# The opening of a diffusion trunk: the first norm's modulation maps computed in two halves of their outputs

## Chip, cores and metric

The kernel runs on one core of a Trainium2 chip. The metric is the device time of one execution in microseconds; lower is better. Where a profile is quoted, it is that of one execution, and its times count from the start of that execution's span.

## What is computed

Two layers of a transformer trunk over 1024 latent tokens and 256 context tokens, with 1024 channels. Layer 0 mixes tokens by neighbourhood attention, layer 1 by sliding-window attention; each layer ends with a gated ConvFFN. The part that matters here is the very first: the modulated norm ahead of layer 0's attention, and the projection to q, k and v behind it.

```python
silu_c, silu_cc = jax.nn.silu(c), jax.nn.silu(c_ctx)
for i in range(DEPTH):
    mod = silu_c @ w_mod[i] + b_mod[i]          # (6*D): shift, scale, gate, twice
    mod_c = silu_cc @ w_mod[i] + b_mod[i]       # the same map for context tokens
    sh1, sc1, gt1, sh2, sc2, gt2 = jnp.split(mod[:, None, :], 6, axis=-1)
    ...
    h = modulate(rmsnorm(x, g_attn[i]), sh1, sc1)        # y * (1 + scale) + shift
    hc = modulate(rmsnorm(ctx, g_attn[i]), sh1c, sc1c)
    ...
    q, k, v = attn_inputs(h, w_in, gq, gk, n_kv)         # h @ w_qkv, head norms
```

So before the first projection the kernel needs two maps of w_mod for layer 0, shift and scale: 1024 inputs by 2048 outputs, 8.4 MB of float32.

## The kernel before

**Layout.** Activations lie with channels on the 128 partitions: 8 channel blocks (`KT`), block k holding channels 128k to 128k + 127, tokens along the free dimension. Tokens come in three chunks (`CH`, line 419): chunk 0 and 1 are 512 latent tokens each, chunk 2 the 256 context tokens. The input is `xs[c]`, the modulated norm `h[c]`. Every operand of a big matmul is split in two float32r parts, hi (a rounded copy, made by ACT or DVE) and lo (the rest, a subtraction on DVE or GpSimd), and each product is three matmuls: hi by hi, lo by hi, hi by lo. In the trace chunk 2's parts are `h0chi` and `h0clo`, chunk 0's `h0hi` and `h0lo`; chunk 1's are made later, by `plan_norm`, from the tile that the trace calls `x` too and with sums named `sums`.

**Weights of the projection** come as slabs (class `Slabs`, lines 509 to 545): slab i of a head pair holds channel blocks 2i and 2i + 1, 384 KB, rows of 3 KB. `load` fetches it into a ring of three buffers (`rpool`, tag `raw`), `hi` makes `whi` on ACT, `lo` makes `wlo` on DVE or GpSimd. The first head pair needs slabs 0 to 3; slab 3 takes the buffer of slab 0, and so its load waits for slab 0's lo part. The rings of `whi` and `wlo` have four places each; the input of chunk 2 lies in two places of `wlo` (line 906: blocks 0 to 3 in one, 4 to 7 in the other), so two of the four slabs' lo parts wait until chunk 2's blocks are done with them.

**The opening** (lines 903 to 975) is ordinary program text under Tile's scheduler. That scheduler lays down one queue per engine at build time: by program order among what it takes to be ready. From the first planner's run on (`sc.run()`, line 1264) the order is fixed by hand instead: `Sched` computes an order of all operations from costs and keys, and `InOrder` (line 67) ties each engine's instructions to it. All instructions that go through `InOrder` carry its line, L79, in the trace, so they are told apart by tile names.

The opening's program order before:

1. Loads on SyncE's queue (SP): chunk 2's input in two transfers, biases and gains, chunk 0's input in four, then `wm` for kt = 0 to 7: each 128 rows of both maps, 1 MB, each row 8 KB in one piece.
2. `stats(2)`, then `stats(0)`: squares on ACT, their sum on DVE (`nsum`), the mean by TensorE (`nps<-invd,nsum`), the inverse root by GpSimd and three small DVE operations, its broadcast over partitions by TensorE (`nps<-dg,ones`), and the multiplication of the input by it, block by block (`x<-x,nps`).
3. The maps: for each kt and each of the two maps `mod_mm` (line 316), four matmuls of 256 outputs into four strips of an accumulator, `mod`; 64 matmuls, which the trace counts as 128 instructions. ACT copies each accumulator (`modsb`), TensorE transposes it (`modt`), DVE adds the bias and folds the gain into the scale (`modc`): `mod_finish`, line 299.
4. Loads: slabs 0 to 2, chunk 1's input in four transfers (x1), `c_row`, `cv`.
5. `apply(2)`: per block x * scale + shift (on ACT for even blocks, on DVE for odd ones), the hi copy (on the other of the two), and the lo part on DVE, or on GpSimd for blocks 3 and 7. Then `slabs.ahead(4)`: load where not done, hi and lo of the four slabs, lo of 0 and 2 on DVE, of 1 and 3 on GpSimd. Then `apply(0)`.

**What comes behind.** `plan_na_qkv` (line 1019) projects token tiles of 128 in the order 8, 9 (context), 0, 1, and so on (`ORDER`, line 423); each is 24 matmuls of 384 outputs, `mm`, in the order of the channel blocks. The first tile thus needs slab 0 for blocks 0 and 1, slab 1 for 2 and 3, and so on. Chunk 1's statistics (`sums`, then `pt<-invd,sums` on TensorE) stand in the same hand-made order, behind the first latent tiles. None of that part's text or costs is touched by the change.

Of the kernel before, what the change touches and what calls it, by code (L numbers as in the profile page):

```python
# [34 lines left out]


WBUFS = 4

class Weave:

    def __init__(self):
        self.jobs = []

    def add(self, gen, rank=0):

        self.jobs.append((rank, gen))
        self.jobs.sort(key=lambda j: j[0])

    def tick(self, n=1):
        for _ in range(n):
            left = []
            for j in self.jobs:
                try:
                    next(j[1])
                    left.append(j)
                except StopIteration:
                    pass
            self.jobs = left  # L60

    def drain(self):
        while self.jobs:
            self.tick()


class InOrder:

# [20 lines left out]
class Sched:  # L89
# [6 lines left out]
                                       pool=(0.15, 0.08, 0.06, 0.1), dma=(0.0, 0.0, 0.0, 0.0)).items()  # L96
# [145 lines left out]
def trunk_kernel(ctx, tc, xperm, xseq, cc, crow, wmod, wmodt, bmod, gnorm, na_wqkv, na_gqk, na_bias, na_wo,  # L242
# [3 lines left out]
    act, dve, pool, pe, dma = [InOrder(tc, e) for e in (nc.scalar, nc.vector, nc.gpsimd, nc.tensor, nc.sync)]  # L246
# [45 lines left out]
    W = Weave()  # L292

    def split(dst_hi, dst_lo, src):
        act.activation(dst_hi, src, AF.Copy)
# [213 lines left out]
    class Slabs:  # L509
# [17 lines left out]

        def get(self, i):
            return [a.rearrange("p (k c) -> p k c", k=2) for a in self.w[i]]

        def ahead(self, n):

            self.n_ahead = n
            for i in range(n):
                if i not in self.raw:
                    self.load(i)
                self.hi(i)
                self.lo(i, "pool" if i % 2 else "dve")
# [362 lines left out]
    with tc.tile_pool(name="x0", bufs=1, reuse_waits="tile") as xp, \  # L901
# [16 lines left out]
        x_load(2, 2)  # L918
        dma.dma_start(bmod_t, bmod)
        dma.dma_start(gn, gnorm)  # L920
        accs = [ps.tile([P, 512], F32, tag="mod", name=f"mod{v}", bufs=2) for v in range(2)]
        raws = []
# [6 lines left out]
        def stats(c):  # L929

            n = CH[c][1]
            nm = Norm(xs[c], n, lw, lambda: ps.tile([P, 512], F32, tag="n", name="nps", bufs=2), dve)
            for k in range(KT + 1):
                nm.square(k)
                yield
            yield from nm.rstd()
            for k in range(KT):
                dve.tensor_tensor(out=xs[c][:, k, :], in0=xs[c][:, k, :], in1=nm.bc[:, :n], op=ALU.mult)
                yield

        def apply(c):
            r = int(c == 2)
            for k in range(KT):
# [8 lines left out]
                yield  # L952
# [24 lines left out]
    fin = ph.enter_context(tc.tile_pool(name="fin0", bufs=1, reuse_waits="tile"))  # L977
    wk = ph.enter_context(tc.tile_pool(name="wk0", bufs=2, reuse_waits="tile"))
# [1526 lines left out]
```

## Time and profile before

| | |
|---|---|
| median of 3 runs | 2797.7 us (2796.82 to 2798.07) |
| the profiled execution | 2796.63 us, of which the span is 2794.9 us |
| mean granted TensorE clock | 0.99 |
| busy: TensorE matmul, VectorE (DVE), ScalarE (ACT), GpSimd (POOL) | 97%, 82%, 61%, 14% of the span |
| DMA | 385.30 MB, mean 138 GB/s |

The busy shares are means over stages with different limits. The page also has the span in 40 slices of 70 us, with a digit for tenths busy; the timeline lists an engine's instructions as start, duration, engine, line, operation, `out<-in`, shapes and count, and in brackets the idle time before it with what ended it. An entry with a count is several instructions in a row. SPq rows are DMA issues: their start is when SyncE got to issue the transfer.

### The profile page before, as it was taken

The page shows a single profiled execution, that of the slowest core. Times are in us where ns is not written, and L with a number is a line of the kernel's source. Part 1 is how long each engine was busy: PE and PEld are TensorE (multiplying, and loading weights), DVE is VectorE, ACT ScalarE, POOL GpSimd, SP SyncE. Part 2 cuts the span into 40 slices and gives each one's busy share as a digit, 9 for nine tenths or more (in the row PEclk, how much of TensorE's full clock was granted, in tenths as well). Part 3 has the DMA queues.
Part 4 walks back from the last instruction along what each step waited for, and adds up shares of the span by engine and source line. Part 5 has one row for each costly group of instructions (what it writes and reads, how often), then busy time and mean ns, then how long its engine had stood idle before and what let it go on. Part 6 is the DMA issues. An engine that isn't in the chain of part 4 may idle for free.

```text
span 2794.9 us, 43305 instructions
## 1 busy us (share of the span) xinstructions
PE 2713.8 (97%) x15496; PEld 2336.0 (84%) x15496; DVE 2290.5 (82%) x5034; ACT 1704.0 (61%) x3111; POOL 385.1 (14%) x550
## 2 busy tenths in 40 slices
PE   5999999998999999999999999999999999999999
PEld 4899999987799988888888888888877788888887
DVE  6888888887778688777886889989978988888767
ACT  4777777776456555556564557677754666566433
POOL 2111111112000000000010035656620000000000
PEclk9999999999999999999999999999999999999999
DMA  6233343335555543333475641233243223324655
GB/s 259 75 121 122 122 127 105 114 114 164 213 168 186 182 140 108 130 121 129 139 253 169 200 142 57 72 96 105 84 155 106 80 98 113 106 88 160 232 173 188
DMA packets 145264, 385.30 MB, mean 138 GB/s; under 512 B 21269, under 2 KB 34069, under 8 KB 143641
## 3 DMA queue, kind: packets, MB, share of 16 engines
q1 hardware_dynamic: 145048, 382.55, 42.0%
q8 instruction: 121, 1.98, 0.3%
q14 instruction: 95, 0.77, 0.1%
HBM read 315.50 MB, written 66.99 MB: 137 GB/s over the span
## 4 chain that ended last, share of the span: by engine, by line
PE 65%; DVE 5%; issue 2%; POOL 1%; DMA 1%; ACT 1%; POOLq 0%; DVEq 0%; SPq 0%; ACTq 0%
PE ua L79 17%; PE dn L79 15%; PE uc L79 13%; PE mm L79 5%; PE ud L79 4%; PE oacc L79 3%; PE pt L79 2%; PE dnc L79 2%; PE pv L79 2%; PE s L79 2%; DVE S L79 1%; DVE x L79 1%; POOL qa L79 0%; DVE wlo L79 0%; DMA c_dram<-cx 0%
## 5 line engine op out<-in xcount | busy, mean ns | idle before, releaser
L79 ACT ACTIVATE whi<-wraw 128x512 fp32r<-128x512 f32 (+1 forms) x264 | 211.9, 803 | 153.6 <-PE uc L79 57.7
L79 DVE TENSOR_TENSOR wlo<-wraw,whi 128x512 fp32r<-128x512 f32 (+1 forms) x264 | 239.9, 909 | 48.5 <-ACT whi L79 48.1
L79 ACT ACTIVATE S<-S,m 128x640 f32<-128x640 f32 (+3 forms) x288 | 221.0, 768 | 59.6 <-DVE m L79 40.1
L79 PE MATMUL dn<-ghi,whi 128*128 128x512 f32 x616 | 239.9, 390 | 0.0
L79 PE MATMUL dn<-ghi,wlo 128*128 128x512 f32 x616 | 239.7, 389 | 0.0
L79 PE MATMUL dn<-glo,whi 128*128 128x512 f32 x616 | 239.6, 389 | 0.0
L79 ACT ACTIVATE whi<-s 128x1024 fp32r<-128x1024 f32 (+1 forms) x120 | 113.2, 943 | 192.8 <-PE uc L79 128.7
L79 POOL TENSOR_TENSOR qy<-qv,mhalf 128x4 f32<-128x4 f32 (+2 forms) x120 | 137.9, 1150 | 545.7 <-DVE qv L79 512.0
L79 PE MATMUL pt<-idr,S 128*128 128x128 f32 x1280 | 189.7, 276 | 7.8 <-DVE S L79 2.9
L79 ACT ACTIVATE ghi<-graw 128x512 fp32r<-128x512 f32 x154 | 96.0, 629 | 151.7 <-PE dn L79 94.9
L79 PE MATMUL mm<-whi,h0hi 128*128 128x384 f32 x512 | 180.5, 353 | 1.6 <-ACT qraw L79 1.6
L79 PEld LDWEIGHTS pt<-idr,S 128*128 128x128 f32 x1280 | 151.5, 142 | 27.4 <-issue 9.8
L79 PE MATMUL mm<-wlo,h0hi 128*128 128x384 f32 x512 | 172.7, 337 | 0.0
L79 DVE TENSOR_TENSOR glo<-graw,ghi 128x512 fp32r<-128x512 f32 x154 | 105.6, 694 | 80.1 <-ACT ghi L79 47.3
L79 ACT ACTIVATE pt<-pt 128x512 f32<-128x512 f32 (+2 forms) x241 | 124.5, 536 | 55.5 <-PE pt L79 53.9
L79 PE MATMUL pv<-pt,v 128*64 128x256 f32 (+1 forms) x1376 | 154.3, 370 | 0.0
L79 DVE TENSOR_TENSOR wlo<-s,whi 128x1024 fp32r<-128x1024 f32 (+1 forms) x120 | 129.6, 1080 | 23.4 <-ACT whi L79 23.1
L79 PE MATMUL ua<-t12hi,whi 128*128 128x512 f32 x352 | 139.0, 395 | 4.9 <-ACT t12hi L79 4.7
L79 PE MATMUL uc<-t34h,whi 128*128 128x512 f32 x352 | 139.6, 397 | 0.5 <-ACT t34h L79 0.5
L79 PE MATMUL ua<-t12lo,whi 128*128 128x512 f32 x352 | 138.4, 393 | 1.4 <-DVE t12lo L79 1.4
L79 PE MATMUL uc<-t34l,whi 128*128 128x512 f32 x352 | 137.7, 391 | 0.9 <-DVE t34l L79 0.9
L79 PE MATMUL ua<-t12hi,wlo 128*128 128x512 f32 x352 | 137.9, 392 | 0.0
(325 smaller groups left out, 8530.6 us busy)
## 6 DMA issues: line engine op xcount, KB each, us to landing
wraw<-in_w_up_dram SPq DMA_DIRECT2D x132, 512.0 KB, 3.8
wmt<-in_wmodt_dram SPq DMA_DIRECT2D x96, 512.0 KB, 4.2
wraw<-in_w_down_dram SPq DMA_DIRECT2D x44, 512.0 KB, 4.0
graw<-g_dram SPq DMA_DIRECT2D x44, 512.0 KB, 4.8
wraw<-in_w_down_dram SPq DMA_DIRECT2D x88, 256.0 KB, 3.1
graw<-g_dram SPq DMA_DIRECT2D x66, 256.0 KB, 2.8
slab<-in_na_wqkv_dram SPq DMA_DIRECT2D x32, 384.0 KB, 3.2
woraw<-in_na_wo_dram SPq DMA_DIRECT2D x24, 512.0 KB, 5.0
```

What stands on the lines that cost most here:

```text
L79: r = f(*a, **k)
```

## The change

The two maps are computed in two halves of their outputs instead of all at once. Half 0 is outputs 0 to 511 of shift and of scale, which are the constants of channel blocks 0 to 3; half 1 the rest. The loads come half by half: for each half 8 tiles of 512 KB, each row of which is two pieces of 2 KB. Slabs 0 and 1 are loaded between the halves, slab 2 behind the second, slab 3 ahead of x1. An accumulator holds one half of both maps, and `mod_half` makes the constants of four blocks from it. `apply` takes a half: four blocks, with the lo parts after each pair. In the program's order half 0's constants, the splits of slabs 0 and 1 and blocks 0 to 3 of chunks 2 and 0 now stand ahead of the maps' second half; behind it stand blocks 4 to 7 of chunk 2, the splits of slabs 2 and 3, the x1 loads, and blocks 4 to 7 of chunk 0. The helper class `Weave` and `Slabs.ahead` go; the statistics are the same `Norm` calls, written out in line.

```diff
-        for kt in range(KT):
-            raw = xp.tile([P, 2, 1024], F32, tag="wm", name=f"wm{kt}", bufs=KT)
-            dma.dma_start(raw.rearrange("p v c -> p (v c)"), wmod[0, kt * P:(kt + 1) * P, 0:2 * D])
-            raws.append(raw)
+        def wm_load(half):
+            for kt in range(KT):
+                raws[half, kt] = xp.tile([P, 2, 512], F32, tag="wm", name=f"wm{half}{kt}", bufs=2 * KT)
+                dma.dma_start(raws[half, kt], wmod[0, kt * P:(kt + 1) * P, 0:2 * D].rearrange(
+                    "p (v c) -> p v c", v=2)[:, :, half * 512:half * 512 + 512])
+
+        wm_load(0)
+        slabs.load(0)
+        slabs.load(1)
+        wm_load(1)
+        slabs.load(2)
+        dma.dma_start(c_row, cr)
...
-        def apply(c):
+        def apply(c, half):
             r = int(c == 2)
-            for k in range(KT):
+            pend = []
+            for k in range(4 * half, 4 * half + 4):
...
-                yield
-                (pool if k % 4 == 3 else dve).tensor_tensor(out=lo, in0=x, in1=hi.bitcast(F32), op=ALU.subtract)
+                pend.append((k, x, hi, lo))
+                if k % 2:
+                    for k_, x, hi, lo in pend:
+                        (pool if k_ % 4 == 3 else dve).tensor_tensor(out=lo, in0=x, in1=hi.bitcast(F32), op=ALU.subtract)
+                    pend = []
...
-        for c in (2, 0):
-            W.add(stats(c))
-            W.drain()
-        for kt in range(KT):
-            for v in range(2):
-                mod_mm(accs[v], kt, raws[kt][:, v, :], kt == 0, kt == KT - 1)
-        for v in range(2):
-            sb = xp.tile([P, 256], F32, tag="modsb", name="modsb0", bufs=2)
-            act.activation(sb, accs[v][:, :256], AF.Copy)
-            W.add(mod_finish(0, v, sb, lambda: ps.tile([P, 512], F32, tag="modt", name="modt", bufs=2)))
-        W.drain()
-        for j in range(3):
-            slabs.load(j)
-        x_load(1, 4)
-        dma.dma_start(c_row, cr)
-        dma.dma_start(cv, conv)
-        W.add(apply(2))
-        W.drain()
-        slabs.ahead(4)
-        W.add(apply(0))
-        W.drain()
+        def mods(half, a, b):
+            for kt in range(a, b):
+                mod_mm(accs[half], kt, raws[half, kt].rearrange("p v c -> p (v c)"), kt == 0, kt == KT - 1)
+
+        def mod_half(half):
+
+            sb = xp.tile([P, 256], F32, tag="modsb", name="modsb0", bufs=2)
+            act.activation(sb, accs[half][:, :256], AF.Copy)
+            tp = ps.tile([P, 512], F32, tag="modt", name="modt", bufs=2)
+            for s in range(2):
+                pe.transpose(tp[:, s * P:(s + 1) * P], sb[:, s * P:(s + 1) * P], idf)
+            yield
+            js = slice(4 * half, 4 * half + 4)
+            for v in range(2):
+                for r in range(2):
+                    src = tp[:, :256].rearrange("p (s g q) -> p g s q", s=2, g=4)[:, 2 * v:2 * v + 2, :, r]
+                    dst = modc[:, 0, r, v, js].rearrange("p (g s) -> p g s", s=2)
+                    dve.tensor_tensor(out=dst, in0=src, in1=bmod_t[:, 0, v, js].rearrange("p (g s) -> p g s", s=2), op=ALU.add)
+            for r in range(2):
+                dve.scalar_tensor_tensor(out=modc[:, 0, r, 1, js], in0=modc[:, 0, r, 1, js], scalar=1.0,
+                                         in1=gn[:, 0, 0, js], op0=ALU.add, op1=ALU.mult)
+
...
+        mods(0, 0, 6)
+        g = nm[0].rstd()
+        next(g)
+        next(g)
+        mods(0, 6, KT)
+        m = mod_half(0)
...
+        split_slab(0, "dve")
+        split_slab(1, "pool")
+        apply(2, 0)
+        times_bc(0, nm[0], 0, 4)
+        apply(0, 0)
+        times_bc(0, nm[0], 4, KT)
+        mods(1, 0, KT)
+        for _ in mod_half(1):
+            pass
+        apply(2, 1)
+        split_slab(2, "dve")
+        split_slab(3, "pool")
         x_load(1, 4)
-        dma.dma_start(c_row, cr)
         dma.dma_start(cv, conv)
-        W.add(apply(2))
-        W.drain()
-        slabs.ahead(4)
-        W.add(apply(0))
-        W.drain()
+        apply(0, 1)
+        slabs.n_ahead = 4
```

`split_slab(i, e)` loads slab i where that isn't done, and makes its hi on ACT and its lo on engine e. `times_bc(c, nm, k0, k1)` multiplies blocks k0 to k1 - 1 of chunk c by the norm's broadcast.

More of the change, by code (lines that the diff above doesn't have):

```diff
@@ L37 @@
 WBUFS = 4
[L39 to L64, printed above, removed]
 class InOrder:
@@ L290, in trunk_kernel @@
     c_row = dpool.tile([2, D], F32, name="c_row")
-    W = Weave()
     def split(dst_hi, dst_lo, src):
@@ L529, in get @@
             return [a.rearrange("p (k c) -> p k c", k=2) for a in self.w[i]]
[L531 to L538, printed above, removed]
         def plan(self, sc, i, key, uses):
@@ L920, in trunk_kernel, with psn, times_bc, split_slab @@
         dma.dma_start(gn, gnorm)
[L921 to L941 removed]
+        raws = {}
+        def wm_load(half):
[3 more added lines that the diff above has]
+                    "p (v c) -> p v c", v=2)[:, :, half * 512:half * 512 + 512])
+        x_load(0, 4)
+        wm_load(0)
[4 more added lines that the diff above has]
+        dma.dma_start(c_row, cr)
+        def psn():
+            return ps.tile([P, 512], F32, tag="n", name="nps", bufs=2)
+        def times_bc(c, nm, k0, k1):
+            for k in range(k0, k1):
+                dve.tensor_tensor(out=xs[c][:, k, :], in0=xs[c][:, k, :], in1=nm.bc[:, :CH[c][1]], op=ALU.mult)
+        def split_slab(i, e):
+            if i not in slabs.raw:
+                slabs.load(i)
+            slabs.hi(i)
+            slabs.lo(i, e)
+        def apply(c, half):
             r = int(c == 2)
[L943 removed]
+            pend = []
+            for k in range(4 * half, 4 * half + 4):
                 x, hi, lo = xs[c][:, k, :], h[c][0][:, k, :], h[c][1][:, k, :]
@@ L965, in trunk_kernel @@
-        W.drain()
-        for j in range(3):
-            slabs.load(j)
+                pend.append((k, x, hi, lo))
[3 more added lines that the diff above has]
+                    pend = []
+        accs = [ps.tile([P, 512], F32, tag="mod", name=f"mod{half}", bufs=2) for half in range(2)]
+        def mods(half, a, b):
+            for kt in range(a, b):
+                mod_mm(accs[half], kt, raws[half, kt].rearrange("p v c -> p (v c)"), kt == 0, kt == KT - 1)
@@ new lines, in trunk_kernel @@
+        nm = {c: Norm(xs[c], CH[c][1], lw, psn, dve) for c in (2, 0)}
+        for k in range(KT + 1):
+            nm[2].square(k)
+        for _ in nm[2].rstd():
+            pass
+        times_bc(2, nm[2], 0, KT)
+        for k in range(KT + 1):
+            nm[0].square(k)
+        mods(0, 0, 6)
[4 more added lines that the diff above has]
+        m = mod_half(0)
+        next(m)
+        for _ in range(3):
+            next(g)
+        for _ in m:
+            pass
```

4 lines of the change are left out of this document (3 added, 1 removed).

## The prediction

> **What bounds the kernel now.** The page first: is TensorE the bound, and where not?
>
> ```profile
> span 2794.9 us, 43305 instructions
> PE   5999999998999999999999999999999999999999
> ```
>
> PE is full in all slices but the first (70 us), where the change lies. Windows of the trace then give the edge of that stage (columns: window, its length, busy us of PE, PEld, DVE, ACT, POOL with counts, granted clock, DMA share, GB/s):
>
> ```profile
> 0.00:60.00 60.00, 29.92 (x198) 20.72 (x199) 39.45 (x91) 27.23 (x50) 11.85 (x14) 0.89 0.77 295
> 100.00:150.00 50.00, 49.32 (x334) 46.06 (x333) 46.46 (x157) 35.74 (x83) 7.58 (x6) 1.00 0.40 127
> ```
>
> From 100 us on PE has 99%, in an order that is written out and stays. So the question is only how many us earlier PE enters its unbroken run; all behind it moves with that. The timeline of PE (start, duration, instruction, idle before and who ended it) shows the entry:
>
> ```profile
> 38.99 0.41 PE L79 MATMUL mm<-whi,h0chi 128*128 128x384 f32 x1 [2.35 <-DVE h0chi L79]
> 52.14 0.69 PE L79 MATMUL mm<-whi,h0chi 128*128 128x384 f32 x1 [4.12 <-ACT whi L79]
> 54.54 0.69 PE L79 MATMUL mm<-wlo,h0chi 128*128 128x384 f32 x1 [1.40 <-POOL wlo L79]
> 64.69 0.95 PE L79 MATMUL pt<-invd,sums 128*128 128x1 f32 x8
> ```
>
> The first matmul of the projection comes at 38.99, but the stream stops for slab 3, whose wlo GpSimd delivers at 54.49; from 54.54 PE runs on. So the entry is **the end of slab 3's split**. Why is that late? DVE, GpSimd and ACT:
>
> ```profile
> 28.49 4.87 DVE L79 TENSOR_TENSOR x<-x,nps 128x512 f32<-128x512 f32 x8 [1.65 <-PE nps L79]
> 36.25 0.24 DVE L79 TENSOR_TENSOR modc<-modt,bmod_t 128x8 f32<-128x8 f32 x2 [2.89 <-PE modt L79]
> 36.88 0.24 DVE L79 SCALAR_TENSOR_TENSOR modc<-modc,gn 128x8 f32<-128x8 f32 x2
> 37.04 0.95 DVE L79 TENSOR_TENSOR wlo<-slab,whi 128x768 fp32r<-128x768 f32 x1
> 41.04 0.28 DVE L79 CAST h0chi<-x 128x256 fp32r<-128x256 f32 x1
> 42.45 1.91 DVE L79 CAST h0chi<-x 128x256 fp32r<-128x256 f32 x1
> 52.75 2.02 DVE L79 TENSOR_SCALAR x<-x,modc 128x512 f32<-128x512 f32 x1
> ...
> 39.57 1.06 POOL L79 TENSOR_TENSOR h0clo<-x,h0chi 128x256 fp32r<-128x256 f32 x1 [14.22 <-ACT h0chi L79]
> 42.20 2.00 POOL L79 TENSOR_TENSOR wlo<-slab,whi 128x768 fp32r<-128x768 f32 x1
> 52.22 2.27 POOL L79 TENSOR_TENSOR wlo<-slab,whi 128x768 fp32r<-128x768 f32 x1 [1.81 <-issue]
> ...
> 51.26 0.83 ACT L79 ACTIVATE whi<-slab 128x768 fp32r<-128x768 f32 x1
> ```
>
> The maps are ready at 37.12 (36.88 + 0.24), and DVE is then busy without a gap to 54.77. A cast that takes 0.28 alone took 1.91 while GpSimd split a slab (42.20 to 44.20), a tensor_scalar 2.02 in the same way: DVE stalls while GpSimd runs. Slab 3's whi stood in ACT's queue behind blocks of the latent chunk. And what set 37.12? SyncE's queue:
>
> ```profile
> SPq L79 <- DMA wm<-in_wmod_dram: 18.2, 8, 3.2
> ...
> 12.98 0.33 SPq L79 DMA_DIRECT2D wm<-in_wmod_dram  x1
> 15.53 0.33 SPq L79 DMA_DIRECT2D slab<-in_na_wqkv_dram  x1
> 25.47 0.33 SPq L79 DMA_DIRECT2D x<-in_xperm_dram  x1
> 27.96 0.33 SPq L79 DMA_DIRECT2D x<-in_xperm_dram  x1
> 31.46 0.33 SPq L79 DMA_DIRECT2D x<-in_xperm_dram  x1
> 34.00 0.26 SPq L79 DMA_DIRECT2D c_row<-cr  x1
> 34.90 0.35 SPq L79 DMA_DIRECT2D cv<-in_conv_dram  x1
> 38.02 0.33 SPq L79 DMA_DIRECT2D slab<-in_na_wqkv_dram  x1
> ```
>
> SP waited eight times for a wm: each issue waits for the landing of the transfer eight places ahead. So the issues date landings: the last x0 at 12.98, the first wm at 15.53, the last at 34.00, slab 0 at 34.90; 2.49 us per 1 MB tile (25.47 to 27.96), once 3.50. Slab 3's own load (38.02) waits for slab 0's split, since it takes its buffer.
>
> **The change part by part.** *Loads.* The same 8.4 MB of wm now come as 16 tiles of 512 KB, whose rows are runs of 2 KB instead of 8. What a run's length costs, from two windows of 10 us (20 to 30, wm; 2730 to 2740, tiles of 256 KB, 2 KB per row):
>
> ```profile
> DMA packets 582, 4.24 MB, mean 424 GB/s; under 512 B 64, under 2 KB 64, under 8 KB 64
> q1 hardware_dynamic: 581, 4.24, 101.5%
> ...
> DMA packets 1588, 2.90 MB, mean 290 GB/s; under 512 B 174, under 2 KB 174, under 8 KB 1587
> q1 hardware_dynamic: 1587, 2.89, 87.9%
> ```
>
> At full share that is 424 / 1.015 = 418 GB/s against 290 / 0.879 = 330: 1.27 times the time per byte. So a 512 KB tile takes 2.49 / 2 x 1.27 = 1.58 us and a half 12.6. The window at 2730 also has stores, so the bounds are 1.24 (no price) and 1.58; I take 1.58, since nothing else in the trace moves 2 KB runs near saturation. Half 0 lands at 13.0 + 12.6 = 25.6; slabs 0 and 1, now ahead of half 1, cost 0.9 each (34.00 to 34.90): 27.4; half 1 at 40.0, or 41.0 with the one slow step (3.50 for 2.49) that the run before shows too. I take 41.0: **seven us later than the last wm now**.
>
> The Trainium skill, "DMA: Bandwidth & Descriptors", Specifications, states line rate from 512 B per transfer on; its section on small descriptors gives about 3 cycles of overhead per packet. By it 2 KB runs would cost some 3.5% more than 8 KB (67 beats for 64 against 259 for 256, an estimate from that page), and half 1 would land some 5 us sooner than in the sum; the two windows don't agree with it.
>
> *First half of the maps.* The 64 matmuls stay 64 (128 instructions).
>
> ```profile
> 23.98 1.08 PE L79 MATMUL mod<-wm,cpad 128*32 128x256 f32 x8
> 28.38 7.32 PE L79 MATMUL mod<-wm,cpad 128*32 128x256 f32 x110
> 34.67 1.03 PE L79 MATMUL mod<-wm,cpad 128*32 128x256 f32 x14
> ```
>
> PE's order put them behind the latent norm's broadcast, at 28.38; if half 0 is put there too, the rest of its 64 instructions ends at about 31, modsb and transposes at 32. That costs nothing: DVE multiplies by the norm until 33.36 (28.49 + 4.87) anyway. Six more small DVE operations for the second set of constants: 0.87 (36.25 to 37.12 for six).
>
> *Work moved ahead.* On DVE from 33.36: constants 0.9, slab 0's wlo 0.9, and blocks 0 to 3 of both chunks. Their price: 36.25 to 54.77 is 18.5; less constants 0.9, two wlo 1.9 and the two stalls under slab splits (1.91 - 0.28 = 1.6, and for the other an estimated 1.5) leaves 12.6, so 6.3 for four of eight blocks. Sum 41.5. Half 1's constants come after, so DVE's backlog is covered by the load; without that cover it would cost what it overhangs. [...] PE gets the first 12 matmuls of context tile 8 done; that shortens nothing, as its order still waits for slab 3.
>
> *Second half.* From the last wm (34.00) to the constants (37.12) took 3.1; the last tile now has 8 instead of 16 instructions at 1.03 / 14: 2.5, so 43.5. The context's last low part on GpSimd: for the first four blocks before, 37.12 to 40.63 (39.57 + 1.06), 3.5, with a wlo of 0.95 in the way: between 2.6 and 3.5, I take 3.0: 46.5. Slab 2's split has no x2 to wait for, and DVE does it beside. Slab 3's load stands ahead of the x1 loads and lands 1.8 behind half 1, at 42.8; its whi fits before 46. Its wlo must wait for the last context block, since it takes the buffer where x2 lay; 2.0 to 2.27 (I take the upper, as DVE works beside it) plus two handovers of 0.05: **48.9**. So 54.54 - 48.9 = 5.6 us earlier.
>
> One wait is new on SP: slab 3's load, in place behind half 1, waits for slab 0's wlo at some 35, and x1 and cv are queued behind it. Five tiles of half 1 are still in flight then, which cover it; x1 lands by 48 and is first read where the sums begin, past 50. The other edits (both statistics written out in line, low parts in pairs) issue the same instructions and cost nothing as long as DVE has work beside them.
>
> What is late next is the second chunk's norm, which PE starts at 64.69 and for which DVE must have the sums:
>
> ```profile
> 62.11 0.69 DVE L79 TENSOR_TENSOR sums<-sums,sq 128x512 f32<-128x512 f32 x1
> 56.75 0.23 DVE L79 COPY v<-qraw 128x128 f32<-128x128 f32 x1 [1.91 <-ACT qraw L79]
> ```
>
> The sums are ready at 62.80, 1.9 ahead. DVE now stalls under slab 3's split to 48.8 and has some 3.4 left of the latent blocks (6.3 less the context's and the small share already done): 52.2, 2.6 earlier than 54.77. Before 56.75 it waited 1.9 for ACT's copy of PE's result, which it no longer does: sums 4.5 earlier, 58.3, against 59.1 for PE. It just holds; where it doesn't, PE waits and the gain falls towards 4.5.
>
> The sum is made in an execution of 2796.63 (span 2794.9); it gives span 2789.3, 2791.0. The median is 1.1 above that execution: **2792.1**.
>
> **The rivals.** *x1 first.* SP's queue is not in program order throughout:
>
> ```profile
> 0.74 0.37 SPq L79 DMA_DIRECT2D cr<-in_crow_dram  x1
> 1.16 0.65 SPq L79 DMA_DIRECT2D cpad<-in_cc_dram  x1
> 36.00:40.00 4.00, 1.50 (x7) 0.83 (x6) 3.56 (x15) 3.80 (x9) 0.43 (x1) 1.00 1.02 408
> ```
>
> cpad's load is written first, but must wait for a memset, and cr's went ahead: what is thought ready goes first. The x1 loads are always ready, slab 3's only after slab 0's split. If they pass it, slab 3 comes 2.1 MB later, 5.1 us at 408 GB/s, and cv 0.4: it lands at 48.3, whi 49.3, wlo 51.5. Gain 3.0: 2794.7; down to 1.5 if its whi is queued behind more of ACT. Against it: SP holds only eight transfers, so its turn for slab 3 comes when the third tile of half 1 has landed, some 5 us after slab 0, and the order may count slab 0 as split by then.
>
> *No price for short runs.* 16 x 1.24 + 1.8 + 13.0 + 1.0 = 35.6. Then DVE's backlog binds: 41.5 + 0.9 + 3.0 + 2.2 = 47.6. Gain 6.9: 2790.8. The two windows speak against it. The rule of the Trainium skill, "DMA: Bandwidth & Descriptors", cited above, speaks for it.
>
> *Early blocks not early.* PE held the map back from 15.53 to 28.38 by its queue order alone. If half 0's transposes are queued behind half 1's matmuls, or DVE's order puts blocks 0 to 3 behind the second constants, all of the 18.5 - 0.9 stands behind 43.5: 61.1 against 54.77, 6.3 slower: 2804.0. It decides as soon as less than 6.4 us (43.5 - 37.1) of DVE's work is done ahead. Against it: half 0 lands 15 us before half 1, and nothing else is ready on DVE then. This is also the case in which the change doesn't do what it says.
>
> **How the numbers follow.** The forecast has 0.46 (2790.7 to 2793.5), x1 first 0.32 (2794.5 to 2796.3), no price 0.14, early blocks not early 0.08. The range leaves out the last case and the ends of x1 first: 2790.2 to 2796.3. A difference under 0.2% (5.6 us, so 2792.1) can't be told from none here. The forecast lies on that line: half of its 0.46 is faster, with 0.13 of no price: 0.36. Slower by over 0.2%: 0.06. The rest, 0.58, is no change.
>
> **What would show it.** Right: SP issues wm at some 1.6 us intervals and the last wm lands near 41; DVE has no gap from 28.5 to 41; slab 3's issue stands ahead of x1; GpSimd ends its wlo near 48.8 and PE runs from there; the sums' matmul comes near 59. Wrong: four x1 issues ahead of slab 3; wm intervals of 1.25; constants of half 0 later than 34; a wait of PE for the sums; or a later window in which PE's idle time grows by what the opening gained.

## The result and the profile after

| | before | changed |
|---|---|---|
| median | 2797.44 us (13 runs, 2796.15 to 2804.68) | 2790.73 us (13 runs, 2787.30 to 2794.33) |
| ratio, 95% interval | | 0.9976 [0.9968, 0.9983] |
| span of the profiled execution | 2794.9 us | 2788.8 us |

The changed kernel is 6.7 us faster, 0.24%. In its trace the operations carry L51. The first lines of the page, then two stretches in the view by windows, whose columns are those of the prediction:

```profile
span 2788.8 us, 43317 instructions
...
PE   6999999998999999999999999999998999999999
...
0.00:60.00 60.00, 33.79 (x234) 23.83 (x235) 43.29 (x106) 28.68 (x54) 13.34 (x16) 0.89 0.80 295
100.00:150.00 50.00, 49.32 (x344) 45.14 (x343) 46.88 (x156) 36.23 (x84) 8.58 (x7) 1.00 0.45 141
```

In the first 60 us TensorE has 33.79 us of work where it had 29.92; from 100 to 150 us it is busy for 49.32 us, to the hundredth as before. So the gain lies in the opening. TensorE's timeline there:

```profile
37.71 0.64 PE L51 MATMUL mod<-wm,cpad 128*32 128x256 f32 x8 [0.69 <-DMA wm<-in_wmod_dram]
42.46 0.69 PE L51 MATMUL modt<-idr,modsb 128*128 128x128 f32 x2 [4.11 <-ACT modsb L51]
42.80 0.67 PE L51 MATMUL mm<-whi,h0chi 128*128 128x384 f32 x1
50.12 0.44 PE L51 MATMUL mm<-wlo,h0chi 128*128 128x384 f32 x1 [1.91 <-POOL wlo L51]
58.57 0.34 PE L51 MATMUL mm<-wlo,h0hi 128*128 128x384 f32 x1
58.95 1.05 PE L51 MATMUL pt<-invd,sums 128*128 128x1 f32 x8
77.06 0.39 PE L51 MATMUL s<-klc,q 128*128 128x256 f32 x1 [1.98 <-ACT klc L51]
```

The last tile of the maps landed at 37.71. The run without a wait begins at 50.12 (54.54 before), the sums' matmul stands at 58.95 (64.69). The first `s<-klc` behind a wait stands at 77.06; it is called the first scores below, though five products of scores run some 2.5 us before it. The trace of before has it so:

```profile
82.70 0.39 PE L79 MATMUL s<-klc,q 128*128 128x256 f32 x1 [1.99 <-ACT klc L79]
```

So 4.42 us are gained at the entry, 5.74 at the sums and 5.64 at the scores, and 6.1 in the span. These three marks serve below: another profile of the changed kernel repeated them within 0.11 us (run `e12_changed_again`), while its span differed by 0.6 us. VectorE, GpSimd and ScalarE around the entry:

```profile
34.93 2.27 DVE L51 TENSOR_SCALAR x<-x,modc 128x256 f32<-128x256 f32 x2
41.39 0.68 DVE L51 TENSOR_TENSOR h0lo<-x,h0hi 128x512 fp32r<-128x512 f32 x1
43.18 0.37 DVE L51 TENSOR_TENSOR modc<-modt,bmod_t 128x4 f32<-128x4 f32 x4 [1.11 <-PE modt L51]
43.52 0.24 DVE L51 SCALAR_TENSOR_TENSOR modc<-modc,gn 128x4 f32<-128x4 f32 x2
48.33 2.02 DVE L51 CAST h0hi<-x 128x512 fp32r<-128x512 f32 x1
50.27 2.98 DVE L51 TENSOR_TENSOR h0lo<-x,h0hi 128x512 fp32r<-128x512 f32 x3
58.21 0.69 DVE L51 TENSOR_TENSOR sums<-sums,sq 128x512 f32<-128x512 f32 x1
...
35.22 1.82 POOL L51 TENSOR_TENSOR wlo<-slab,whi 128x768 fp32r<-128x768 f32 x1 [10.08 <-ACT whi L51]
42.21 1.27 POOL L51 TENSOR_TENSOR h0lo<-x,h0hi 128x512 fp32r<-128x512 f32 x1 [3.56 <-ACT h0hi L51]
46.20 1.92 POOL L51 TENSOR_TENSOR h0clo<-x,h0chi 128x256 fp32r<-128x256 f32 x1 [2.73 <-ACT h0chi L51]
48.20 1.86 POOL L51 TENSOR_TENSOR wlo<-slab,whi 128x768 fp32r<-128x768 f32 x1
...
41.50 0.63 ACT L51 ACTIVATE h0hi<-x 128x512 fp32r<-128x512 f32 x1 [2.63 <-DVE x L51]
42.04 0.37 ACT L51 ACTIVATE modsb<-mod 128x256 f32<-128x256 f32 x1
45.72 0.40 ACT L51 ACTIVATE h0chi<-x 128x256 fp32r<-128x256 f32 x1
```

VectorE works on the early blocks to 42.07 (41.39 + 0.68). The copy of the second accumulator, `modsb`, whose matmuls had ended at 38.35, stood on ScalarE behind a rounding that waited for VectorE, and left at 42.04; so the second constants begin at 43.18. From there GpSimd's two low parts lead to 50.06, 0.06 ahead of TensorE's entry. The sums are ready at 58.90, 0.05 ahead of their matmul. TensorE's matmul before that one had begun at 58.57, and in this run one begins every 0.17 us: so TensorE stood some 0.2 us for the sums, which came last there. On SyncE:

```profile
35.04 0.35 SPq L51 DMA_DIRECT2D slab<-in_na_wqkv_dram  x1
35.45 1.86 SPq L51 DMA_DIRECT2D x<-in_xperm_dram  x4
```

Slab 3's load left ahead of x1's four.

### The profile page after: what moved, and what is told of

Read it like the earlier page. It is cut to its first block, busy times and chain, and to the rows that moved or that the text cites. A ratio compares the mean times of both kernels' runs of the same rounds, so it can differ in the third digit from the quotient of the medians.

```text
span 2788.8 us, 43317 instructions
## 1 busy us (share of the span) xinstructions
PE 2710.8 (97%) x15496; PEld 2331.8 (84%) x15496; DVE 2290.1 (82%) x5040; ACT 1703.7 (61%) x3111; POOL 383.1 (14%) x550
## 4 chain that ended last, share of the span: by engine, by line
PE 83%; DVE 6%; issue 3%; POOL 2%; ACT 1%; DMA 1%; POOLq 0%; DVEq 0%; ACTq 0%
PE ua L51 17%; PE dn L51 15%; PE mm L51 15%; PE uc L51 13%; PE pt L51 5%; PE pv L51 5%; PE s L51 4%; PE ud L51 4%; PE oacc L51 3%; PE dnc L51 2%; DVE S L51 1%; DVE wlo L51 1%; DVE x L51 1%; POOL qa L51 0%; ACT S L51 0%
## 5 line engine op out<-in xcount | busy, mean ns | idle before, releaser
L51 ACT ACTIVATE whi<-wraw 128x512 fp32r<-128x512 f32 (+1 forms) x264 | 212.0, 803 | 152.8 <-PE uc L51 57.4
L51 DVE TENSOR_TENSOR wlo<-wraw,whi 128x512 fp32r<-128x512 f32 (+1 forms) x264 | 240.7, 912 | 47.3 <-ACT whi L51 46.8
L51 ACT ACTIVATE S<-S,m 128x640 f32<-128x640 f32 (+3 forms) x288 | 221.0, 768 | 57.7 <-DVE m L51 39.3
L51 PE MATMUL dn<-ghi,whi 128*128 128x512 f32 x616 | 240.2, 390 | 0.0
L51 PE MATMUL dn<-ghi,wlo 128*128 128x512 f32 x616 | 239.9, 390 | 0.0
L51 PE MATMUL dn<-glo,whi 128*128 128x512 f32 x616 | 239.9, 389 | 0.0
L51 ACT ACTIVATE whi<-s 128x1024 fp32r<-128x1024 f32 (+1 forms) x120 | 113.2, 943 | 193.0 <-PE uc L51 117.9
L51 POOL TENSOR_TENSOR qy<-qv,mhalf 128x4 f32<-128x4 f32 (+2 forms) x120 | 136.7, 1139 | 546.4 <-DVE qv L51 512.7
L51 PE MATMUL pt<-idr,S 128*128 128x128 f32 x1280 | 189.8, 277 | 7.8 <-DVE S L51 3.3
L51 ACT ACTIVATE ghi<-graw 128x512 fp32r<-128x512 f32 x154 | 96.0, 629 | 150.3 <-PE dn L51 96.2
L51 PE MATMUL mm<-whi,h0hi 128*128 128x384 f32 x512 | 181.0, 354 | 1.6 <-ACT qraw L51 1.6
L51 PEld LDWEIGHTS pt<-idr,S 128*128 128x128 f32 x1280 | 151.6, 142 | 26.9 <-issue 9.9
L51 PE MATMUL mm<-wlo,h0hi 128*128 128x384 f32 x512 | 172.7, 337 | 0.0
L51 DVE TENSOR_TENSOR glo<-graw,ghi 128x512 fp32r<-128x512 f32 x154 | 106.2, 698 | 81.0 <-ACT ghi L51 48.4
L51 ACT ACTIVATE pt<-pt 128x512 f32<-128x512 f32 (+2 forms) x241 | 124.5, 536 | 56.6 <-PE pt L51 55.1
L51 PE MATMUL pv<-pt,v 128*64 128x256 f32 (+1 forms) x1376 | 154.7, 371 | 0.0
L51 DVE TENSOR_TENSOR wlo<-s,whi 128x1024 fp32r<-128x1024 f32 (+1 forms) x120 | 129.8, 1081 | 23.3 <-ACT whi L51 23.0
L51 PE MATMUL ua<-t12hi,whi 128*128 128x512 f32 x352 | 139.1, 395 | 4.9 <-ACT t12hi L51 4.7
L51 PE MATMUL uc<-t34h,whi 128*128 128x512 f32 x352 | 139.7, 397 | 0.5 <-ACT t34h L51 0.5
L51 PE MATMUL ua<-t12lo,whi 128*128 128x512 f32 x352 | 138.6, 394 | 1.4 <-DVE t12lo L51 1.4
L51 PE MATMUL uc<-t34l,whi 128*128 128x512 f32 x352 | 137.9, 392 | 0.9 <-DVE t34l L51 0.9
L51 PE MATMUL ua<-t12hi,wlo 128*128 128x512 f32 x352 | 138.1, 392 | 0.0
```

What stands on the lines that cost most here:

```text
L51: r = f(*a, **k)
```

## The experiments

**The theories.** *VectorE's queue:* the gain is VectorE's work on the early blocks, done while half 1 still loads; what VectorE has left decides when the sums come. *The entry:* the gain is the earlier split of slab 3, and the early blocks only fill idle time. Two smaller terms could stand in either: the price of the short runs, and TensorE's clock. In the run from the entry to chunk 0's first matmul (28 matmuls), the kernel before took 6.52 us (54.54 to 61.06) and the changed one 4.99 (50.12 to 55.11). The granted clock, third from the end of these rows of the view by windows, of before and of the changed kernel, says why:

```profile
52.00:56.00 4.00, 2.47 (x7) 1.96 (x8) 2.84 (x4) 1.24 (x3) 2.76 (x2) 0.50 0.12 17
```

```profile
52.00:56.00 4.00, 4.00 (x25) 4.00 (x25) 3.69 (x9) 3.97 (x10) 0.00 (x0) 1.00 0.49 194
```

Before, TensorE started its run at half clock. Marks of all kernels, in us, with the ratio of the times (for e1 to e12 against the kernel before on the same chip):

| run | entry | sums ready | sums' matmul | first scores | ratio to before, 95% interval |
|---|---|---|---|---|---|
| before | 54.54 | 62.80 | 64.69 | 82.70 | |
| changed | 50.12 | 58.90 | 58.95 | 77.06 | 0.9976 [0.9968, 0.9983] |
| e12, changed again | 50.22 | 59.00 | 59.06 | 77.17 | 0.9977 [0.9968, 0.9986] |
| e1, runs alone | 56.08 | 64.33 | 65.96 | 83.97 | 1.0000 [0.9991, 1.0010] |
| e2, late blocks | 48.66 | 62.40 | 62.45 | 82.94 | 1.0006 [0.9997, 1.0016] |
| e3, slab 3 first | 47.76 | 61.71 | 61.77 | 79.88 | 0.9990 [0.9981, 0.9999] |
| e4, warm PE | 54.57 | 62.36 | 63.17 | 81.17 | 0.9993 [0.9983, 1.0002] |
| e5, copy ahead | 49.94 | 58.71 | 60.22 | 78.23 | 0.9985 [0.9976, 0.9995] |
| e6, slab 3's lo on DVE | 49.38 | 58.23 | 58.28 | 76.39 | 0.9981 [0.9972, 0.9990] |
| e7, e5 and e6 | 49.12 | 58.40 | 59.35 | 77.36 | 0.9980 [0.9970, 0.9989] |
| e8, x1 first | 52.88 | 61.13 | 63.60 | 81.61 | 1.0000 [0.9990, 1.0009] |
| e9, x1 first, order kept | 51.21 | 59.47 | 61.16 | 79.16 | 0.9985 [0.9976, 0.9994] |
| e10, e5 with filler | 50.11 | 58.88 | 60.27 | 78.29 | 0.9986 [0.9976, 0.9995] |
| e11, low parts on DVE | 48.67 | 57.93 | 60.06 | 78.06 | 0.9974 [0.9963, 0.9986] |

The intervals are some 2.6 us to either side, so the times tell apart differences of 3 us, not of one; below that the marks of the trace speak. Mark and time agree as far as that goes: the shift of the first scores against before and the shift of the time that the ratio gives (of 2797 us) differ by at most 1.5 us, but for e11 (4.6 against 7.3, with the widest interval).

**e1: the half loads alone.** The kernel before with `wm` loaded half by half, all matmuls, constants and blocks where they were.

```diff
-            raw = xp.tile([P, 2, 1024], F32, tag="wm", name=f"wm{kt}", bufs=KT)
-            dma.dma_start(raw.rearrange("p v c -> p (v c)"), wmod[0, kt * P:(kt + 1) * P, 0:2 * D])
+        for half in range(2):
+            for kt in range(KT):
+                raws[half, kt] = xp.tile([P, 2, 512], F32, tag="wm", name=f"wm{half}{kt}", bufs=2 * KT)
+                dma.dma_start(raws[half, kt], wmod[0, kt * P:(kt + 1) * P, 0:2 * D].rearrange(
+                    "p (v c) -> p v c", v=2)[:, :, half * 512:half * 512 + 512])
```

> The kernel before, with only the loads of wm changed: 16 tiles of 512 KB in runs of 2 KB, first half, then second half; the order of all work stays. This prices the short runs by themselves. As predicted (1.58 us a tile): the last wm lands at 13.0 + 16 x 1.58 = 38.3 instead of 34.0, the maps end some 4 us later, and the time rises by about 4 us. As the trace of the changed kernel shows them (1.35 us a tile, 16.95 to 18.30): the last wm lands at 34.6, and the time rises by less than 1 us.

Its last tile of the maps landed at 35.22 where before had 34.00, and the entry moved by 1.54. The DMA view gives the rates, 20 to 24 us, of before and of the changed kernel:

```profile
DMA packets 224, 1.70 MB, mean 424 GB/s; under 512 B 17, under 2 KB 17, under 8 KB 17
```

```profile
DMA packets 746, 1.56 MB, mean 391 GB/s; under 512 B 60, under 2 KB 60, under 8 KB 746
```

424 / 391 is 1.08; e1 itself has 387 GB/s there, which gives 1.10. So runs of 2 KB cost 8 to 10% against runs of 8 KB, not 27%, and the shorter runs by themselves give nothing.

**e2: the blocks not early.** The changed kernel, with half 0's constants held back until half 1's accumulator is done, and the early blocks written behind them. The loads and the slabs keep the new order.

```diff
+            if half == 0:
+                z = xp.tile([P, 1], F32, name="zero")
+                dve.tensor_scalar(out=z, in0=accs[1][:, 0:1], scalar1=0.0, scalar2=None, op0=ALU.mult)
+                act.activation(sb, accs[0][:, :256], AF.Identity, bias=z)
...
+        for half in range(2):
+            for _ in mod_half(half):
+                pass
+        split_slab(0, "dve")
+        split_slab(1, "pool")
+        apply(2, 0)
...
+        apply(0, 0)
         apply(0, 1)
```

> The changed kernel, with half 0's constants held until half 1's accumulator is done as well (its copy takes a bias of zero that is made from the other accumulator), and the splits of slabs 0 and 1 and blocks 0 to 3 written behind both. Loads, slab order and x1's place stay. If the early blocks are what gains, because DVE is the bound up to the second chunk's sums: DVE has its whole 18 us from about 40 on, the sums' matmul comes at 64 to 65 where the changed kernel has 58.95, and the time is that of before within 2 us (2796 to 2799). If the gain lies in slab 3's place ahead of x1 and of the latent blocks: PE still enters its unbroken run near 50, and the time stays within 1.5 us of the changed kernel's 2790.7.

```profile
48.66 0.44 PE L51 MATMUL mm<-wlo,h0chi 128*128 128x384 f32 x1 [0.51 <-POOL wlo L51]
62.45 1.86 PE L51 MATMUL pt<-invd,sums 128*128 128x1 f32 x8 [3.66 <-DVE sums L51]
82.94 0.39 PE L51 MATMUL s<-klc,q 128*128 128x256 f32 x1 [1.99 <-ACT klc L51]
```

TensorE enters 1.5 us earlier than in the changed kernel, and still the gain is gone: it then waits 3.66 us for VectorE's sums, and the first scores stand 0.24 us behind those of before. Not all of that is the sums. At their matmul e2 is still 2.24 us ahead of the kernel before (62.45 for 64.69); behind the wait TensorE ran at half clock, as the granted clock of e2 shows:

```profile
62.00:66.00 4.00, 3.54 (x14) 3.55 (x15) 2.28 (x11) 0.47 (x1) 3.37 (x3) 0.50 0.16 37
66.00:70.00 4.00, 4.00 (x22) 3.97 (x21) 2.14 (x11) 1.35 (x5) 1.01 (x1) 0.80 0.16 61
```

From the sums' matmul to the first scores e2 took 20.49 us, the changed kernel 18.11. So of the 5.88 us between the two at the scores 3.50 are the later sums, and 2.38 were lost behind the wait for them. An early entry without early blocks was worth nothing at the scores here; e3 shows that it need not be nothing.

**e3: slab 3's load first, nothing else.** The kernel before, with the x1 loads, and `cv` behind them, moved behind `slabs.ahead(4)`.

```diff
-        x_load(1, 4)
         dma.dma_start(c_row, cr)
-        dma.dma_start(cv, conv)
         W.add(apply(2))
         W.drain()
         slabs.ahead(4)
+        x_load(1, 4)
+        dma.dma_start(cv, conv)
```

> The kernel before with one thing moved: the x1 loads stand behind slab 3's load, so that slab 3 lands some 5 us earlier and its split can come ahead of the latent blocks. Maps whole, runs of 8 KB. If slab 3's place is the whole gain: PE enters its unbroken run at 47 to 48 and the time falls by 6 to 7 us, as in the changed kernel. If DVE is the bound behind it: PE enters as early, but then waits for latent blocks and sums, which DVE ends no more than 2 us earlier than before; the sums' matmul comes at 61 to 62 and the time falls by 3 to 4 us.

```profile
47.76 0.69 PE L79 MATMUL mm<-wlo,h0chi 128*128 128x384 f32 x1 [1.48 <-DVE wlo L79]
61.77 1.05 PE L79 MATMUL pt<-invd,sums 128*128 128x1 f32 x8 [2.15 <-DVE sums L79]
```

The entry is 6.8 us earlier, more than the change gains, but at the first scores 2.8 are left (82.70 to 79.88), because the sums come only 1.1 earlier. Of the entry's gain in the kernel before, VectorE lets less than half through. TensorE's wait for the sums was 2.15 us here and the granted clock 1.00 from 62 to 66 us, so that part was kept, where e2 lost it.

The two runs together decide between the theories. Without early blocks, and with an entry 5.9 or 6.8 us earlier, the sums' matmul comes 2.24 (e2) or 2.92 us (e3) earlier than before; with them it comes 5.74 earlier, though the entry gains only 4.42. So the earlier entry alone is good for two fifths to a half of the gain at that mark, and VectorE's work on the early blocks for the rest.

**e4: the clock.** The kernel before with 24 matmuls added, whose result nothing reads, in TensorE's idle time from 47.80 to 53.53.

```diff
+    idle = psa("pv", F32)
+    for k in range(1, 7):
+        for _ in range(4):
+            pe.matmul(idle, idr, h[0][0][:, k, :], start=True, stop=True)
```

> The kernel before plus 24 matmuls whose result nobody reads, on latent blocks 1 to 6, placed where PE waits for slab 3 (47.9 to 54.5). This asks what PE's slow start is worth: in the kernel before the 28 matmuls from 54.54 to the first latent one at 61.06 took 6.52 us, in the changed one, where PE had run without a long gap from 42.8, the same 28 took 4.99 (50.12 to 55.11). If the long idle time is the cause: entry unchanged at 54.5, the 28 take about 5.0, the sums' matmul comes at 63.2, and the time falls by about 1.5 us. If not: they take 6.5 again and nothing changes.

The entry stays (54.57); the sums' matmul comes at 63.17 in place of 64.69 and the first scores 1.53 earlier. So a warm start of the run is worth 1.5 us in the trace. The time moved by 0.07%, with an interval that holds 1.

**e5, e6, e7: what bounds the changed kernel.** e5 puts the copy of the second accumulator ahead of the rounding it stood behind; e6 makes slab 3's low part on VectorE; e7 does both.

```diff
-        apply(0, 0)
-        times_bc(0, nm[0], 4, KT)
+        apply(0, 0, 2)
         mods(1, 0, KT)
-        for _ in mod_half(1):
-            pass
+        m = mod_half(1)
+        next(m)
+        apply(0, 0, 2, 2)
+        times_bc(0, nm[0], 4, KT)
+        for _ in m:
+            pass
...
-        split_slab(3, "pool")
+        split_slab(3, "dve")
```

In `e5` and `e7` block 3's rounding is also tied behind the copy on ScalarE. The first `next(m)` makes only the copy; the last pair of lines is `e6`.

> The changed kernel with one wait taken from ScalarE's queue: the copy of the second half's accumulator (modsb) goes ahead of chunk 0's rounding of channel block 3, behind which it stood until 42.04 while its accumulator was done near 39. If VectorE's work on the early blocks (to 42.07 in the changed kernel's trace) is what the second constants wait for, they start at 42.1 in place of 43.18, every later mark (the sums' matmul at 58.95, the first s<-klc at 77.06) comes 1.1 us earlier, and the span is 2787.7 against 2788.8. If GpSimd's chain behind them (the last context block, then slab 3's low part, to 50.06) takes none of it, the marks move by less than 0.3.

> The changed kernel with slab 3's low part on VectorE (0.95 us in its rows) in place of GpSimd (1.86 us). If TensorE's entry decides, it comes near 48.4 in place of 50.12 and the sums' matmul and the first s<-klc 1.7 us earlier (57.3 and 75.4). If VectorE's queue decides, it gains only what its CAST of h0hi loses beside GpSimd today (2.02 against 0.42 us) less the 0.95 added: the sums' matmul waits for sums and stands near 58.3, the first s<-klc near 76.4, 0.6 us earlier.

> Both edits, the copy ahead on ScalarE and slab 3's low part on VectorE. With VectorE as the bound 1.1 + 0.6 = 1.7 us below the changed kernel at the first s<-klc (75.4) and in the span (2787.1); with TensorE's entry as the bound 2.8 (74.3, 2786.0); nothing if neither queue is what the marks wait for.

e6 came out where VectorE's queue was to put it (sums' matmul 58.28 for 58.3, first scores 76.39 for 76.4). But it doesn't separate the two theories: VectorE reached slab 3's split only at 48.39, the entry came at 49.38 and not near 48.4, and that is 0.74 earlier too. Sums and TensorE were again within 0.1 us of each other. Its time can't be told from the changed kernel's. e5 fell for both theories: the marks came 1.2 us *later*. Its rows, TensorE, then VectorE and GpSimd:

```profile
44.66 0.45 PE L51 MATMUL mm<-whi,h0chi 128*128 128x384 f32 x1 [2.77 <-DVE h0chi L51]
47.19 0.52 PE L51 MATMUL mm<-whi,h0chi 128*128 128x384 f32 x1
47.51 0.52 PE L51 MATMUL mm<-whi,h0clo 128*128 128x384 f32 x1
...
60.22 0.95 PE L51 MATMUL pt<-invd,sums 128*128 128x1 f32 x8
...
42.31 1.26 DVE L51 SCALAR_TENSOR_TENSOR modc<-modc,gn 128x4 f32<-128x4 f32 x2
...
42.21 1.27 POOL L51 TENSOR_TENSOR h0lo<-x,h0hi 128x512 fp32r<-128x512 f32 x1 [3.56 <-ACT h0hi L51]
```

Two things account for it. The constants did begin 1.2 us early (41.99), but their scale, 0.24 us in the changed kernel, took 1.26, to the end of GpSimd's low part (42.21 + 1.27): the changed kernel's wait of 1.11 had only covered that stall, and 0.19 us were left. And the tile 8 matmuls, now early, left TensorE idle for 2.77 us, then for 0.21 and 0.96; behind these waits its matmuls came 0.32 us apart (47.19, 47.51) where the changed kernel has 0.17. It entered its run at half clock (granted clock 0.50 from 48 to 52 us). The sums were ready at 58.71, but TensorE was late for them. e7 shows the second again: sums at 58.40, matmul at 59.35.

**e8, e9: the first rival made true.** x1's loads ahead of slab 3's. Beside the lines shown, e8 ties the rounding of chunk 0's block 5 and the low part of its block 7 behind slab 3's split; the scheduler then put the other rounding of that half ahead of slab 3's. e9 ties both roundings, and that low part, behind it.

```diff
         split_slab(2, "dve")
-        split_slab(3, "pool")
         x_load(1, 4)
+        split_slab(3, "pool")
```

> The changed kernel with chunk 1's four loads issued ahead of slab 3's, the order of the prediction's first rival; the rounding of slab 3 keeps its place on ScalarE and GpSimd. As that rival was priced, entry moves by 2 to 3 us and the time by 2.6. By the changed kernel's trace slab 3 would land near 45 in place of 39, and its rounding does not start before 46.03: entry stays at 50.1 within 0.3, and the span at 2788.8 within 0.5.

> Chunk 1's four loads again issued ahead of slab 3's, as in the run before it, where the planner had also put slab 3's rounding on ScalarE behind chunk 0's rounding of a later block (50.05 in place of 46.03 in the changed kernel). Here both roundings of chunk 0's second half are tied behind slab 3's, so only the loads change places. If the transfer is what the prediction's first rival lost by, entry still moves by 2 to 3 us and the first s<-klc from 77.06 to 79 or later. If it was ScalarE's order, slab 3's rounding stands within 1 us of 46.03, and entry (50.12) and the first s<-klc within 0.7 of the changed kernel's.

e8's entry came 2.8 us late: its `whi` of slab 3 started at 50.05, from ScalarE's queue, not from the transfer; at the first scores 4.55 of the 5.64 us were lost. In e9 it started at 46.92, without a wait, as expected; but the entry moved by 1.1 and the first scores by 2.1, more than expected:

```profile
51.21 0.69 PE L51 MATMUL mm<-wlo,h0chi 128*128 128x384 f32 x1 [2.54 <-POOL wlo L51]
51.70 0.52 PE L51 MATMUL mm<-whi,h0chi 128*128 128x384 f32 x1
52.02 0.52 PE L51 MATMUL mm<-whi,h0clo 128*128 128x384 f32 x1
...
46.38 2.84 POOL L51 TENSOR_TENSOR h0clo<-x,h0chi 128x256 fp32r<-128x256 f32 x1 [2.71 <-ACT h0chi L51]
49.30 1.86 POOL L51 TENSOR_TENSOR wlo<-slab,whi 128x768 fp32r<-128x768 f32 x1
```

GpSimd's low part of the context took 2.84 us in place of 1.92, with another order of VectorE's work beside it, and behind the longer wait (2.54 in place of 1.91) TensorE was at half clock again. So e9 met neither of its two forecasts whole. The rival's size was about right (2.1 us in the marks for 2.6 predicted; the medians of e9 and e12 are 1.75 apart, less than the times tell apart), by another path than its transfer.

**e10, e11: filler, and VectorE alone.** e10 is e5 with eight unread matmuls behind tile 8's first twelve; e11 is e10 with four low parts on VectorE that GpSimd had after 42 us: slab 3's, the context's block 7 and chunk 0's blocks 3 and 7.

```diff
+                if J["id"] == ("q0", 0, 8) and kt == 3:
+                    idle = psa("pv", F32)
+                    for _ in range(8):
+                        pe.matmul(idle, idr, h[0][0][:, 1, :], start=True, stop=True)
...
-                        (pool if k_ % 4 == 3 else dve).tensor_tensor(out=lo,
+                        (pool if (c, k_) == (2, 3) else dve).tensor_tensor(out=lo,
```

> The copy-ahead edit with eight unread 128x512 matmuls added on TensorE behind context tile 8's first twelve, so that TensorE doesn't stand idle for 2.77 us ahead of channel block 4. If the half clock was what made the copy-ahead kernel late (its run from 46.73 to 53.3 at a spacing of 0.32), the spacing is 0.17 throughout, and the sums' matmul waits for VectorE's sums alone: 58.7 in place of 60.22, the first s<-klc near 76.9 in place of 78.23. It then gains only 0.2 on the changed kernel, because VectorE spends the 1.1 us won in the scale constant's 1.26 us instruction beside GpSimd's h0lo. If it was not the clock, the marks stay at 60.2 and 78.2.

> The kernel with the copy ahead and the unread matmuls, and with slab 3's low part and the three low parts of h that GpSimd had after 42 us on VectorE too. VectorE has then some 2.8 us more of its own work after 42.07 and none of its instructions stretched by GpSimd (CAST 2.02 for 0.42, h0lo 2.98 for 1.9, the constant 1.26 for 0.24, and the 1.1 us wait gone). Worked out from the changed kernel's rows its additions of squares start near 51.9 in place of 53.38: sums' matmul near 57.5 in place of 58.95, first s<-klc near 75.6, span near 2787.4. If GpSimd's work doesn't stretch VectorE's, this kernel is later than the changed one by up to 1.5 us.

> The changed kernel itself, on the same chip as the three others, to see how far its marks repeat: entry 50.12, the sums' matmul 58.95 and the first s<-klc 77.06 within 0.4 each if marks of one profile can carry differences of half a microsecond; its span within 1.5 of 2788.8.

The filler didn't keep the clock, so e10 doesn't answer its question: waits of 1.13, 0.21 and 0.96 us were left between 43.69 and 46.89, and from there the spacing was 0.32 again. That the clock is what the early tile costs is thus read from the granted clock and the spacings of e5, and from the price in e4; e10 doesn't show it. In e11 VectorE did about what was expected, TensorE not:

```profile
48.67 0.69 PE L51 MATMUL mm<-wlo,h0chi 128*128 128x384 f32 x1 [0.52 <-DVE wlo L51]
49.16 0.52 PE L51 MATMUL mm<-whi,h0chi 128*128 128x384 f32 x1
60.06 0.95 PE L51 MATMUL pt<-invd,sums 128*128 128x1 f32 x8
...
57.24 0.69 DVE L51 TENSOR_TENSOR sums<-sums,sq 128x512 f32<-128x512 f32 x1
```

With some 2.8 us more work of its own, VectorE had the sums at 57.93, 0.97 *earlier* than in the changed kernel and 0.95 earlier than in e10, which has the same edits but for the four low parts: the stalls beside GpSimd's four low parts had cost VectorE more than doing them itself. But TensorE entered at half clock (0.50 from 48 to 54 us) and came to the sums at 60.06. No version here beats the changed kernel by more than the measurement can tell.

## Why the prediction was right

The time was predicted as 2792.1 us and came out at 2790.73; the sums' matmul was to stand at 59.1 and stood at 58.95. The mechanism is the one that was put forward, an earlier entry with VectorE's work done ahead, while half 1 loads; e2 and e3, which lack the early blocks, keep 2.24 and 2.92 of the 5.74 us at the sums' matmul. The cover was shorter than forecast: half 1's accumulator was done at 38.35 and the early work ended at 42.07, so its last 3.7 us held back the second constants. Several steps were off, and two of them cancelled; that the mark agrees to 0.15 us is luck.

- *Loads.* The step "a 512 KB tile takes 1.58 us" was mis-sized. From one tile's landing to the next it took 1.33 us (36.38 to 37.71 in TensorE's waits), and the last landed at 37.71 in place of 41.0. The window at 2730 us, from which 27% came, has stores in it, as the text said; the price is 8 to 10%. The rule of the Trainium skill, "DMA: Bandwidth & Descriptors", Specifications and the section on small descriptors, from which 3.5% were estimated, was nearer to it, and lower than the runs show.
- *First half of the maps.* Right: it lay under the multiplications by the norm, and VectorE had no gap until 42.07.
- *Work moved ahead.* The backlog was put at 41.5 and ended at 42.07. The sum had no stall for slab 1's split on GpSimd (35.22 to 37.04), but two operations on 128x256 took 2.27 us beside it (34.93), where two took 0.73 in the kernel before (37.91). The blocks themselves took 6.0 us, where 6.3 were put. "PE gets the first 12 matmuls of context tile 8 done" was wrong: TensorE's queue had the transposes of the second half ahead of them, and they waited for ScalarE's copy to 42.46.
- *Second half.* The constants were put at 43.5 and stood at 43.76 (43.52 + 0.24), for another reason than the load: VectorE's backlog, and ScalarE's order behind it. The context's low part was put at 46.5 and ended at 48.12 (46.20 + 1.92): I took 3.0 us from the constants on, between 2.6 and 3.5; it took 4.4. Of the 1.4 us between, 0.9 are GpSimd's instruction, 1.06 before and 1.92 now, with other work of VectorE beside it. The other 0.5 had been taken off for a slab split that was not on the path: GpSimd began 2.44 us behind the constants (46.20), as before (2.45, at 39.57), both times behind ScalarE's roundings, which ran without a gap. This is the step that failed in the entry, 48.9 predicted and 50.12 measured; slab 3's split, 1.86 for 2.27, took some of it back.
- *The run behind the entry.* A term was missing: TensorE's clock. Tile 8's late start at 42.80 and a wait of only 1.91 us kept it up, and the run to chunk 0 took 4.99 us in place of 6.52. This gave back 1.5 us where the entry had lost 1.2; that is why the sums' matmul agrees to 0.15.
- *What is late next.* "It just holds" was right to 0.2 us, for which TensorE waited: the sums were ready at 58.90, 0.6 later than put. That VectorE holds an earlier entry back there is what e2 and e3 show, with waits of 3.66 and 2.15 us.
- *SyncE.* Slab 3's load went ahead of x1, so the largest rival didn't come about. e9 puts it at 2.1 us, where it had 2.6. Its lower end, slab 3's rounding queued behind more of ScalarE, is what e8 became: a gain of 1.09 us at the first scores, where it had 1.5.
- *No price for short runs:* half of its premise held (8% is nearer to none than to 27%), and its conclusion that VectorE's backlog then binds held too. Its entry at 47.6 did not, by the same step of the context's low part.
- *Early blocks not early:* e2 made it so. It was priced at 6.3 us slower; e2 was at 1.0006 [0.9997, 1.0016], and its first scores 0.2 later than before. Two terms of the price were too high: the second constants, put at 43.5, came at 40.85 in e2, as the load was cheaper; and VectorE needed 15.0 us behind them (to 55.84), not 17.6, with slab 0's split done ahead of them. One term was missing: the 2.38 us lost behind the wait for the sums, at half clock, are in e2's first scores.

What stays open: why the span gained 6.1 us where the scores gained 5.64. Spans of two profiles of one kernel differed by 0.6, so there may be nothing behind it. Open too: what in VectorE's work makes GpSimd's low part take 1.06, 1.92 or 2.84 us; no run takes that work away.

## What to carry to other kernels

An entry point of the busiest engine is a good mark only if nothing behind it waits for another queue: look for the next wait, and ask whether the engine that ends it has gained as much. A wait that one means to remove may be the cover of a stall, or may keep the next stretch together so that TensorE's clock stays up; both are seen only when the instructions behind it are followed to their new places. A price taken from a window with other traffic in it should be kept as an upper bound, and the forecast put nearer to the clean rows.

## What the runs showed of the hardware

- *TensorE's clock falls after short waits too.* After a single wait of 1.91 us it stayed up (the changed kernel, granted clock 1.00 from 48 to 56 us). It fell with waits of 1.13, 0.21 and 0.96 within 3.2 us (e10), and in e11 with waits of 2.03, 0.23 and 0.52 within 4.8 us. The Trainium skill, "TensorE: Matmul & The Clock Gate", Part 1, ties the half clock to at least one idle window of some 3.4 us that runs freely; no wait just ahead of the fall was that long in those two kernels, so an unbroken wait of that length wasn't needed. What decides instead, these runs don't show. A cold start of the run behind the entry cost 1.5 us (e4).
- *VectorE is stretched beside GpSimd.* Beside GpSimd a CAST of 0.42 us took 2.02, and two instructions on 4 columns took 1.26 in place of 0.24; in e11, without GpSimd beside them, they were short again (0.42; 0.16 and 0.15 each). GpSimd's 128x256 subtraction took 1.06, 1.92 or 2.84 us, with different work of VectorE beside it each time.
- *Runs of 2 KB moved at 391 GB/s, runs of 8 KB at 424,* on one core from 20 to 24 us, within the loads of the maps.
